# Row-wise infinity norm: the last 16 results of each partition leave in one store at the end, in place of an early store and a last one

## Chip, cores, metric

One NeuronCore of a Trainium2 chip. The metric is the device time of one execution in microseconds (us); lower is better. Before the change it was 628.59 us (median of 3 runs, 628.57 to 628.78).

## The reference

```python
x: float32 [8192, 8192]
return np.linalg.norm(x, ord=np.inf, axis=1)      # the largest |x| of each row
```

So 268.44 MB are read, 32 KB are written, and every element is looked at once.

## The kernel before

Each of the 128 partitions owns 64 rows. The first 48 of them ("bulk") come in 24 loads of two rows per partition; VectorE reduces each load to two numbers. The last 16 ("tail") come in loads of shrinking size, so that little is left to do when the last bytes arrive. All loads are issued by SP (the SyncE engine); ACT is ScalarE. A transfer reports its end by raising a semaphore, which engines wait for; "landing" below is the moment at which that semaphore is complete.

```python
TAIL = [[2944, 13440], [4096, 12288], [11520, 4864], ...,          # cut
        [2432, 2176, 1920, 1664, 1536, 1280, 1152, 1024, 1152, 1024, 1024]]
...
r_bulk = outp.tile([P, A, G * B], F32)
r_tail = outp.tile([P, n_tail], F32)           # n_tail = 16
r_fin = outp.tile([P, 1], F32)
part = outp.tile([P, n_tail - 1, k_max], F32)
nc.vector.memset(part[:], 0.0)
def absmax(o, i):
    nc.vector.reduce_max(out=o, in_=i, axis=X, apply_absolute_value=True)
...
nc.scalar.dma_start(out=out_b, in_=r_bulk[:])      # bulk results
for i, loads in enumerate(TAIL):
    t = sbuf.tile([P, W + PAD], F32, tag="t")
    ...
    for j, w in enumerate(loads):
        nc.sync.dma_start(out=t[:, at : at + w], in_=x_t[i][:, at : at + w])
        ...
            if r < n_tail - 1:
                absmax(part[:, r, k : k + 1], t[:, lo : lo + n])
                if r == n_tail - 2 and k == count[r] - 1:
                    absmax(r_tail[:, : n_tail - 1], part[:])
                    nc.scalar.dma_start(out=out_t[:, : n_tail - 1],
                                        in_=r_tail[:, : n_tail - 1])
            elif k < n_last - 1:
                absmax(t[:, W + k : W + k + 1], t[:, lo : lo + n])
            else:
                absmax(r_fin[:], t[:, lo : W + n_last - 1])
nc.sync.dma_start(out=out_t[:, n_tail - 1 :], in_=r_fin[:])
```

15 of a partition's tail results are combined and stored while the last row still arrives (128 runs of 60 bytes, on ACT's queue); the 16th is stored alone at the end (128 runs of 4 bytes, on SP's queue).

Of the kernel before, what the change touches and what calls it, by code (L numbers as in the profile page):

```python
# [1 line left out]
logging.getLogger("concourse").setLevel(logging.ERROR)  # L3

# [1 line left out]

# [4 lines left out]

F32 = mybir.dt.float32
X = mybir.AxisListType.X



TAIL = [
    [2944, 13440],
    [4096, 12288],
    [11520, 4864],  # L20
    [7680, 8704],
    [6528, 3328, 6528],
    [4864, 4096, 3328, 4096],
    [3968, 3584, 3328, 2944, 2560],
    [2432, 2176, 1920, 1664, 1536, 1280, 1152, 1024, 1152, 1024, 1024],
]


def segments(loads, cols):

    out, at = [], 0
    for i, w in enumerate(loads):
        end = at + w
        while at < end:
            r = at // cols
            to = min(end, (r + 1) * cols)
            out.append((i, r, at - r * cols, to - at))
            at = to
    return out


def start_first_load_early(nc):


    sp = mybir.EngineType.SP
    first, *rest = nc.main_func.blocks
    for block in rest:
        insts = block.instructions
        for i, ins in enumerate(insts):
            if ins.engine == sp and type(ins).__name__ == "InstDMACopy":  # L50
                assert not ins.sync_info.on_wait
                moved = insts[i]
                block.instructions = insts[:i] + insts[i + 1 :]
                head = first.instructions
                at = next(k for k, h in enumerate(head) if h.engine == sp)
                first.instructions = head[:at] + [moved] + head[at:]
                return


@with_exitstack  # L60
def kernel(
    ctx: ExitStack,
    tc: tile.TileContext,
    x: bass.AP,
    out: bass.AP,
    G: int = 4,
    B: int = 2,
    BUFS: int = 3,
    PAD: int = 16,
):  # L70
    nc = tc.nc
    P = nc.NUM_PARTITIONS
    rows, cols = x.shape
    W = B * cols


    n_tail = B * len(TAIL)
    n_bulk_rows = rows // P - n_tail
    assert n_bulk_rows % (G * B) == 0
    A = n_bulk_rows // (G * B)  # L80
    split = n_bulk_rows * P
    x_b = x[:split].rearrange("(a p n b) c -> a n p (b c)", p=P, a=A, n=G, b=B)
    out_b = out[:split].rearrange("(a p n b) -> p a (n b)", p=P, a=A, n=G, b=B)
    x_t = x[split:].rearrange("(p t b) c -> t p (b c)", p=P, b=B)
    out_t = out[split:].rearrange("(p t) -> p t", p=P)

    sbuf = ctx.enter_context(tc.tile_pool(name="sbuf", bufs=BUFS))
    outp = ctx.enter_context(tc.tile_pool(name="outp", bufs=1))

    segs = [segments(loads, cols) for loads in TAIL]  # L90
    count = {}
    for i, s in enumerate(segs):
        for _, r, _, _ in s:
            count[i * B + r] = count.get(i * B + r, 0) + 1
    n_last = count[n_tail - 1]
    k_max = max(count[r] for r in range(n_tail - 1))
    assert n_last - 1 <= PAD

    r_bulk = outp.tile([P, A, G * B], F32)
    r_tail = outp.tile([P, n_tail], F32)  # L100
    r_fin = outp.tile([P, 1], F32)
    part = outp.tile([P, n_tail - 1, k_max], F32)
    nc.vector.memset(part[:], 0.0)  # L103

    def absmax(o, i):
        nc.vector.reduce_max(out=o, in_=i, axis=X, apply_absolute_value=True)  # L106

    for a in range(A):
        for n in range(G):
            t = sbuf.tile([P, W + PAD], F32, tag="t")  # L110
            nc.sync.dma_start(out=t[:, :W], in_=x_b[a, n])
            absmax(
                r_bulk[:, a, n * B : (n + 1) * B],
                t[:, :W].rearrange("p (b c) -> p b c", b=B),
            )
    nc.scalar.dma_start(out=out_b, in_=r_bulk[:])

    seen = {}
    for i, loads in enumerate(TAIL):
        t = sbuf.tile([P, W + PAD], F32, tag="t")  # L120
        todo = segs[i]
        at = 0
        for j, w in enumerate(loads):
            nc.sync.dma_start(out=t[:, at : at + w], in_=x_t[i][:, at : at + w])  # L124
            at += w
            for _, b, c, n in [s for s in todo if s[0] == j]:
                r = i * B + b
                k = seen.get(r, 0)
                seen[r] = k + 1
                lo = b * cols + c  # L130
                if r < n_tail - 1:
                    absmax(part[:, r, k : k + 1], t[:, lo : lo + n])
                    if r == n_tail - 2 and k == count[r] - 1:

                        absmax(r_tail[:, : n_tail - 1], part[:])
                        nc.scalar.dma_start(
                            out=out_t[:, : n_tail - 1], in_=r_tail[:, : n_tail - 1]
                        )
                elif k < n_last - 1:
                    absmax(t[:, W + k : W + k + 1], t[:, lo : lo + n])  # L140
                else:

                    absmax(r_fin[:], t[:, lo : W + n_last - 1])
    nc.sync.dma_start(out=out_t[:, n_tail - 1 :], in_=r_fin[:])
    nc.at_finalize(start_first_load_early)


# [1 line left out]
_INS = ['x']  # L149
_OUTS = [((8192,), 'float32')]  # L150


# [23 lines left out]
```

## Time and profile before

| before | |
|---|---|
| time | 628.59 us |
| profiled span | 627.3 us |
| bytes over the span | 428 GB/s, DMA nine tenths busy or more in 39 of 40 slices |
| VectorE (DVE) busy | 88% |
| end of VectorE's last reduction | 625.02 us |
| from there to the end of the span | 2.29 us |

Lines of the page's first parts (others left out): busy time by engine, then forty slices of the span with the busy tenths of each engine and of the DMA.

```profile
span 627.3 us, 201 instructions
DVE 553.0 (88%) x64; POOL 0.2 (0%) x4
DVE  0688998888988889888898888998889999999998
DMA  9999999999999999999999999999999999999997
DMA packets 8994, 268.49 MB, mean 428 GB/s; under 512 B 1952, under 2 KB 1952, under 8 KB 3104
```

The DMA is full to the last slice, and VectorE is nearly full in the last quarter. How full, the windows show: start and end of a stretch, its length, DVE's busy time, then POOL, clock, DMA share and GB/s.

```profile
560.00:597.30 37.30, 37.10 (x11) 0.00 (x0) 1.00 1.00 426
597.30:615.70 18.40, 18.37 (x8) 0.00 (x0) 1.00 1.00 422
615.70:625.03 9.33, 9.26 (x8) 0.00 (x0) 1.00 0.74 300
625.03:627.30 2.27, 0.00 (x0) 0.00 (x0) 1.00 0.03 0
```

VectorE idles 0.1 us in the last 28 us of its work. The instructions of the end in order of time (start, duration, engine, line, operation, out<-in):

```profile
611.69 2.30 SPq L124 DMA_DIRECT2D t<-in_x_dram  x2
615.73 0.22 DVE L106 TENSOR_REDUCE r_tail<-part 128x15 f32<-128x60 f32 x1
615.86 7.90 DVE L106 TENSOR_REDUCE t<-t 128x1 f32<-128x1536 f32 x6
615.97 0.35 ACTq L136 DMA_DIRECT2D out_dram<-r_tail  x1
623.80 1.23 DVE L106 TENSOR_REDUCE r_fin<-t 128x1 f32<-128x1030 f32 x1
625.05 0.35 SPq L144 DMA_DIRECT2D out_dram<-r_fin  x1
```

The issues of stores, with KB and us from issue to landing:

```profile
out_dram<-r_bulk ACTq DMA_DIRECT2D x1, 24.0 KB, 60.1
out_dram<-r_tail ACTq DMA_DIRECT2D x1, 7.5 KB, 5.3
out_dram<-r_fin SPq DMA_DIRECT2D x1, 0.5 KB, 1.4
```

The early store (r_tail) overlaps VectorE's work and the loads. The last one (r_fin) begins when VectorE is done, and nothing overlaps it.

### The profile page before, as it was taken

To read this page: it belongs to the slowest core of one execution; us is meant where nothing else is said; L and a number is where in the kernel's file an instruction comes from. 1 tells how busy PE (TensorE), PEld (TensorE's weight loads), DVE (VectorE), ACT (ScalarE), POOL (GpSimd) and SP (SyncE) were. 2 spreads that over 40 slices of the span, in tenths; PEclk is the share of its full clock that TensorE was granted. 3 is DMA by queue.
4 is the path that set the end of the run, shared out by engine and by line. 5 is a ranking of instruction groups with operands and counts; after the bars stand their busy time and mean duration, and the time that the engine had idled before them with its cause. 6 is when DMAs were issued, how large, how long until landed. Compare 5 with 4: busy or idle time off the path is not lost.

```text
span 627.3 us, 201 instructions
## 1 busy us (share of the span) xinstructions
DVE 553.0 (88%) x64; POOL 0.2 (0%) x4
## 2 busy tenths in 40 slices
DVE  0688998888988889888898888998889999999998
POOL 0000000000000000000000000000000000000000
DMA  9999999999999999999999999999999999999997
GB/s 401 468 401 468 401 468 401 464 405 455 414 451 418 451 418 401 468 401 468 401 468 401 468 401 468 401 468 401 468 418 406 460 430 410 436 422 430 428 423 287
DMA packets 8994, 268.49 MB, mean 428 GB/s; under 512 B 1952, under 2 KB 1952, under 8 KB 3104
## 3 DMA queue, kind: packets, MB, share of 16 engines
q1 hardware_dynamic: 8064, 268.44, 99.3%
q10 hardware_dynamic: 928, 0.03, 0.1%
q14 instruction: 2, 0.02, 0.0%
HBM read 268.44 MB, written 0.03 MB: 428 GB/s over the span
## 4 chain that ended last, share of the span: by engine, by line
DMA 67%; DVE 28%; another core or an unknown queue 4%; SPq 0%; issue 0%
DMA t<-in_x_dram 67%; DVE r_bulk L106 22%; DVE part L106 5%; DVE t L106 1%; DVE r_fin L106 0%; SPq L124 0%; DVE r_tail L106 0%
## 5 line engine op out<-in xcount | busy, mean ns | idle before, releaser
L106 DVE TENSOR_REDUCE r_bulk<-t 128x2 f32<-128x16384 f32 x24 | 413.3, 17220 | 70.1 <-DMA t<-in_x_dram 70.1
L106 DVE TENSOR_REDUCE part<-t 128x1 f32<-128x8192 f32 (+18 forms) x31 | 130.5, 4273 | 0.9 <-DMA t<-in_x_dram 0.6
L106 DVE TENSOR_REDUCE t<-t 128x1 f32<-128x1152 f32 (+3 forms) x6 | 7.9, 1387 | 0.0
L106 DVE TENSOR_REDUCE r_fin<-t 128x1 f32<-128x1030 f32 x1 | 1.2, 1226 | 0.0
L103 DVE MEMSET part<- 128x60 f32 x1 | 0.1, 108 | 0.9 <-PEq L160 0.9
L106 DVE TENSOR_REDUCE r_tail<-part 128x15 f32<-128x60 f32 x1 | 0.2, 216 | 0.0
L160 POOL MEMSET const-bfloat16-1.0<- 128x1 bf16 x1 | 0.1, 103 | 0.0
L160 POOL MEMSET const-uint8-127<- 128x1 uint8 x1 | 0.1, 103 | 0.0
L160 POOL MEMSET const-float32-1.0<- 128x1 f32 x1 | 0.1, 100 | 0.0
L160 POOL MEMSET const-float32-0.0<- 128x1 f32 x1 | 0.1, 99 | 0.2 <-issue 0.2
## 6 DMA issues: line engine op xcount, KB each, us to landing
t<-in_x_dram SPq DMA_DIRECT2D x1, 6720.0 KB, 40.4
t<-in_x_dram SPq DMA_DIRECT2D x2, 3264.0 KB, 26.4
t<-in_x_dram SPq DMA_DIRECT2D x3, 2048.0 KB, 29.0
t<-in_x_dram SPq DMA_DIRECT2D x1, 6144.0 KB, 40.6
t<-in_x_dram SPq DMA_DIRECT2D x1, 5760.0 KB, 35.3
t<-in_x_dram SPq DMA_DIRECT2D x3, 1664.0 KB, 32.5
t<-in_x_dram SPq DMA_DIRECT2D x2, 2432.0 KB, 32.6
t<-in_x_dram SPq DMA_DIRECT2D x1, 4352.0 KB, 42.8
```

The costliest lines, as they stand in the source:

```text
L103: nc.vector.memset(part[:], 0.0)
L106: nc.vector.reduce_max(out=o, in_=i, axis=X, apply_absolute_value=True)
L160: nc = _bacc.Bacc("TRN2", target_bir_lowering=False, num_devices=1)
```

## The change

The intent: one store where there were two, in whole 64-byte runs, and no store among the last loads.

```diff
-    r_fin = outp.tile([P, 1], F32)
 ...
                         absmax(r_tail[:, : n_tail - 1], part[:])
-                        nc.scalar.dma_start(
-                            out=out_t[:, : n_tail - 1], in_=r_tail[:, : n_tail - 1]
-                        )
 ...
-                    absmax(r_fin[:], t[:, lo : W + n_last - 1])
-    nc.sync.dma_start(out=out_t[:, n_tail - 1 :], in_=r_fin[:])
+                    absmax(r_tail[:, n_tail - 1 :], t[:, lo : W + n_last - 1])
+    nc.sync.dma_start(out=out_t, in_=r_tail[:])
```

## The prediction

> **What bounds the kernel.** It streams 268.44 MB through 16 DMA engines: the page's slices show DMA at nine tenths or more in all but the last, 428 GB/s over the 627.3 us span. VectorE is 88% busy. In the bulk it waits about 2.1 us for each load (70.1 us in all, groups of instructions). From 519.67 us that turns: its tail reductions run nearly back to back (windows: 37.10 of 37.30 us from 560.0, 18.37 of 18.40 from 597.3, 9.26 of 9.33 from 615.7). So the end is VectorE's chain, then one store: the chain of waits ends with the 1.23 us reduction into r_fin at 623.80; the store issues at 625.05 (DMA issues: 1.4 us to landing; in the trace its first packet moves 0.85 us after the issue starts and its semaphore is complete at 626.30); then 1.0 us of closing semaphores and drains.
>
> **What the change does.**
> - Removed: the early store of 15 results (ACT's queue, 128 runs of 60 bytes, issued at 615.97, landed 5.3 us later, among the loads). No VectorE instruction waits for it. Its packets took 11 ns each, some 0.09 us on each of 16 DMA engines (estimate, 8 x 11 ns). The last load could land about 0.1 us earlier. It landed at 623.60, while VectorE was busy with the reduction before until 623.76: worth 0.
> - Moved: those 60 bytes into the last store. Same issuing engine, same 128 runs, 64 bytes each in place of 4. A 4-byte packet took 7 to 9 ns, a 60-byte one 11 ns; with 8 in series on each engine the store grows by an estimated 0.02 to 0.03 us, all on the critical path.
> - Unchanged: every reduction, also the 0.22 us one of the partial results, and the closing sequence. The last reduction writes column 15 of r_tail in place of r_fin: same shape, 1.23 us.
> - Side effect: completion semaphores are used in rotation (eight in the trace), so without the early store the last loads should each wait for a load one earlier, and issue up to 2 us sooner. The load queue is never empty there (410 to 422 GB/s from 616 to 622 us, windows): nothing gained.
>
> The Trainium skill ("DMA: Bandwidth & Descriptors", "Anatomy of one DMA") puts a small DMA's cost mostly in a fixed part, about 2 us, dominated by the write receipt. The trace agrees that it is fixed, at 1.24 us from issue to semaphore for 512 bytes, though most of that lies ahead of the first packet. The page's specifications say that transfers below 512 B are read-modify-written; 4, 60 and 64 bytes all are, so I expect little from longer runs: any gain must come out of the 0.2 us between last packet and semaphore.
>
> **Prediction.** +0.03 us for bytes, at most -0.05 us for whole pieces, 0 for the removed store. Time 628.6 us, 8 in 10 between 628.0 and 629.2. Chances: faster by over 2% 0.5%, within 2% 99%, slower by over 2% 0.5%.
>
> **What would show it.** Right: the last reduction ends within 0.2 us of 625.03; the last store takes 1.3 to 1.5 us to landing; packets under 512 B fall by 144 (128 data, 16 for the semaphore). Wrong: a last store of over 1.6 us, or VectorE finishing earlier (it did wait for disturbed loads).
>
> **What would make it wrong.** A load that lands later because issues move, so that VectorE waits at the end (slack is only 0.16 us at the last load); a last store that waits for something besides the last reduction; run-to-run drift, which at 628.57 to 628.78 exceeds the effect.

## The result

| | before | after |
|---|---|---|
| median, us | 628.63 (6 runs, 628.43 to 629.10) | 628.60 (6 runs, 628.33 to 629.41) |
| profiled span, us | 627.3 | 626.8 |

The ratio is 1.0001, with a 95% interval of 0.9988 to 1.0014: the same. (A ratio here is the mean time of one kernel's runs over that of the other's of the same rounds, so it isn't quite the ratio of the medians quoted.) Later the changed kernel ran again for five rounds: 0.9996 (0.9983 to 1.0008). The four that ran once (e5, e8, e9, e10): only stretches within their traces are read.

The profile after, the same views:

```profile
span 626.8 us, 199 instructions
DVE 552.9 (88%) x64; POOL 0.2 (0%) x4
DVE  0588988889988889888898888998889999999998
DMA  9999999999999999999999999999999999999997
DMA packets 8850, 268.49 MB, mean 428 GB/s; under 512 B 1808, under 2 KB 1808, under 8 KB 2960
```

```profile
611.24 0.33 SPq L123 DMA_DIRECT2D t<-in_x_dram  x1
615.27 0.22 DVE L105 TENSOR_REDUCE r_tail<-part 128x15 f32<-128x60 f32 x1
615.41 7.91 DVE L105 TENSOR_REDUCE t<-t 128x1 f32<-128x1536 f32 x6
623.35 1.23 DVE L105 TENSOR_REDUCE r_tail<-t 128x1 f32<-128x1030 f32 x1
624.60 0.35 SPq L140 DMA_DIRECT2D out_dram<-r_tail  x1
```

```profile
out_dram<-r_tail SPq DMA_DIRECT2D x1, 8.0 KB, 1.4
```

VectorE is as full in the stretch before the last row as it was before the change, and the only wait for a tail load that the view lists is the same early one of 0.6 us (total us, times, longest):

```profile
597.30:615.70 18.40, 18.37 (x10) 0.00 (x0) 1.00 1.01 423
DVE part L105 <- DMA t<-in_x_dram: 0.6, 1, 0.6
```

Small packets fell by 144 (1952 to 1808), as they should: 128 of data and 16 for a semaphore. The last store takes 1.4 us, with sixteen times the bytes. The profiled span is 0.51 us shorter, but that is not the change's doing: the first tail reduction starts 0.27 us sooner (484.02 against 484.29 us), more than 100 us ahead of the first instruction that differs; another 0.18 us arises in VectorE's short waits for loads between there and the last reduction, and is scatter: from the first tail reduction to the end of the last took 140.74 us before and 140.56 after, but 140.45 in a later run with the early store (e1_both) and 140.70 in one without it (e6_bulk_late). Only 0.06 us lies behind the last reduction (2.23 us to the end of the span in place of 2.29). What those 0.06 us are is a question that the prediction had not foreseen.

### The profile page after: what moved, and what is told of

Read it like the earlier page. It is cut to its first block, busy times and chain, and to the rows that moved or that the text cites. A ratio compares the mean times of both kernels' runs of the same rounds, so it can differ in the third digit from the quotient of the medians.

```text
span 626.8 us, 199 instructions
## 1 busy us (share of the span) xinstructions
DVE 552.9 (88%) x64; POOL 0.2 (0%) x4
## 2 busy tenths in 40 slices
DMA packets 8850, 268.49 MB, mean 428 GB/s; under 512 B 1808, under 2 KB 1808, under 8 KB 2960
## 4 chain that ended last, share of the span: by engine, by line
DMA 67%; DVE 28%; another core or an unknown queue 4%; SPq 0%; issue 0%
DMA t<-in_x_dram 67%; DVE r_bulk L105 22%; DVE part L105 5%; DVE t L105 1%; DVE r_tail L105 0%; SPq L123 0%
```

## The experiments

Twelve kernels ran. Exact intervals below are differences of the trace's records; "behind the last reduction" is from the end of VectorE's last reduction to the end of the span.

**The theory.** VectorE's chain sets when the last store starts; the early store only delays loads, within VectorE's slack at the last load; the last store has a fixed cost, and its bytes weigh 0.02 us. **Rivals**: (1) two effects cancel, a gain from dropping the early store and a cost of the wider last one; (2) whole 64-byte runs land faster than 4-byte ones; (3) stores among the loads are free whatever their size.

### One half of the change at a time

The control, the changed kernel itself (e0_after):

> Control: the changed kernel again, in the rounds of the next three. Both theories: 628.6 us, within 0.15% of the kernel before. In its trace the last store takes 1.4 us to landing.

Measured: 628.56 us against 628.71 us of before on that chip, ratio 0.9996.

Both stores, with the last one wide (e1_both), against the changed kernel:

```diff
+                        nc.scalar.dma_start(
+                            out=out_t[:, : n_tail - 1], in_=r_tail[:, : n_tail - 1]
+                        )
```

> The early store of 15 results is kept, and the last store carries all 16 (64-byte runs). Theory (both halves are worth about nothing): within 0.15% of before; from the end of the last reduction to the end of the span 2.25 to 2.35 us, as in before (2.28) and after (2.24). Rival 1 (two effects cancel: the wider last store costs what the dropped early store gains): slower than before, with the span's end over 0.2 us later after the last reduction. Rival 2 (whole 64-byte pieces land faster than 4-byte ones): last store under 1.2 us to landing in place of 1.4.

Measured: 628.62 us, ratio 0.9998 (0.9985 to 1.0010).

Only the early store dropped (e2_no_early), against the kernel before; its output is wrong:

```diff
-                        nc.scalar.dma_start(
-                            out=out_t[:, : n_tail - 1], in_=r_tail[:, : n_tail - 1]
-                        )
```

> The early store is dropped and the last stays at 4-byte runs, so 15 of the 16 tail rows are never written: wrong on purpose. Theory: within 0.15% of before; the last load lands 0.2 to 0.3 us before VectorE is done with the reduction ahead of the last (0.17 in before), and VectorE does not use it. Rival 1: faster by what the early store cost, with VectorE's last reduction ending over 0.2 us sooner after the combining reduction's start (9.31 us in before).

Measured: 628.62 us, ratio 0.9998 (0.9984 to 1.0012). The four kernels side by side, from the traces:

| | early store | last store, bytes a run | last load lands ahead of VectorE by | issue to last semaphore step | behind the last reduction |
|---|---|---|---|---|---|
| before | yes | 4 | 0.17 us | 1.41 us | 2.29 us |
| e1_both | yes | 64 | 0.16 us | 1.41 us | 2.30 us |
| e2_no_early | no | 4 | 0.26 us | 1.42 us | 2.23 us |
| after | no | 64 | 0.24 us | 1.41 us | 2.23 us |

This settles most of it. Each effect goes with one half of the change and does not depend on the other, so nothing cancels (rival 1 falls). The width of the last store makes no difference that can be seen (rival 2 falls for 128 runs). Dropping the early store brings the last load about 0.08 to 0.09 us forward, which is the 0.09 us that the prediction estimated from 8 packets of 11 ns, and VectorE, still at the reduction before, does not use it. (The last load is also issued 2 us sooner without the early store, and these runs do not part the two. But it lies in the queue for 9.9 us before and 11.8 us after, from issue to landing, with the DMA full, so the earlier issue can hardly be what brought it forward.) And the 0.06 us behind the last reduction go with the early store, not with the width.

### Ten times the dose of the early store

```diff
+                        nc.scalar.dma_start(      # scr: a scratch tensor in HBM; t_prev: the tile before
+                            out=scr.rearrange("p (r k) -> p r k", k=512)[:, :4, :256],
+                            in_=t_prev[:, :2048].rearrange("p (r k) -> p r k", k=512)[:, :, :256],
+                        )
```

> The kernel before with a second early store on ACT's queue, of 512 KB (128 partitions x 4 runs of 1 KB) into a scratch tensor: the early store's suspected cost, transport on the 16 engines, at some ten times the dose. Theory (a store among the loads delays the last load by its transport time, and costs what exceeds VectorE's slack of 0.17 us): 32 runs of about 40 ns on each engine, the last load 0.8 to 1.3 us later, VectorE idle 0.6 to 1.1 us in the tail, 629.3 to 629.7 us. Rival 3 (a store among the loads is off the critical path whatever its size): 628.6 us and no idle time of VectorE in the tail.

Measured: 629.92 us against 628.71, ratio 1.0018 (1.0006 to 1.0031). The schedule issued the store at 588.5 us, earlier than intended, since its source was ready. VectorE's waits of this run, and those of before:

```profile
DVE part L106 <- DMA t<-in_x_dram: 1.7, 5, 0.6
```

```profile
DVE part L106 <- DMA t<-in_x_dram: 0.6, 1, 0.6
```

(total us, times, longest.) VectorE waits 1.1 us more for loads, in four pieces between 597 and 608 us (0.43, 0.20, 0.21 and 0.22 us). So a store among the loads is not free, and rival 3 falls. An estimate of its transport is 1.23 us (0.52 MB at the 425 GB/s of that stretch), and nearly all of it reached VectorE: at 597 us VectorE had no backlog to hide it.

The store had a second effect, though. SP's next load shared its semaphore, and SP waited 13.6 us for it, from 593.2 us on, before issuing any more loads. That could have starved the DMA, but did not: in those 13.6 us the DMA share was 1.02 at 424 GB/s (1.01 and 425 before). So the delay is put down to transport. The measured time is 0.2 us over the expected range; the store was placed where there is no slack at all, and 0.1 us of it is behind the last reduction (2.39 us), for which see the section after next. The 60-byte store was harmless by its size and place, not by its kind.

### How far the last reduction is from its load

The combining reduction (0.22 us) is left out, so 15 tail rows leave as zeros, wrong (e7_no_combine):

```diff
+    nc.vector.memset(r_tail[:], 0.0)
 ...
-                        absmax(r_tail[:, : n_tail - 1], part[:])
+                        pass
```

> The changed kernel without the combining reduction of 0.22 us, so that 15 tail rows leave as zeros: wrong on purpose. Theory (the tail is VectorE's chain, with the last load only 0.17 to 0.24 us ahead of it): the last reduction ends 0.15 to 0.22 us sooner after the start of the first reduction of the last row, measured from the landing of the last load it starts 0.0 to 0.1 us after it; 628.4 us, not clear of noise in the times. Rival 6 (the tail waits for loads): no reduction ends sooner.

Measured: 628.39 us, ratio 0.9993 (0.9978 to 1.0008), not clear of noise. The trace:

```profile
615.26 5.53 DVE L106 TENSOR_REDUCE t<-t 128x1 f32<-128x1536 f32 x4
621.26 2.48 DVE L106 TENSOR_REDUCE t<-t 128x1 f32<-128x1152 f32 x2 [0.47 <-DMA t<-in_x_dram]
623.77 1.23 DVE L106 TENSOR_REDUCE r_tail<-t 128x1 f32<-128x1030 f32 x1
```

VectorE now runs into a load that isn't there yet and waits 0.47 us. Its last reduction starts 0.10 us after the last load's landing, as expected, and ends 1.33 us after it, in place of 1.50 us in the changed kernel: 0.17 us, not 0.22. The other measure, from the first reduction of the last row, is 0.57 us longer and was badly chosen: in this run that reduction itself started early and the wait came behind it. So rival 6 is half right: loads and VectorE end within about 0.2 us of each other. In the last row, taking 0.22 us of work from VectorE alone gained 0.17 us, and taking the early store's 0.09 us from the loads alone (e2_no_early) gained nothing.

### What the 0.06 us are

The closing sequence on SP waits for the loads' and stores' semaphores, eight in rotation, in fixed pairs, one instruction each. SP's closing waits in the trace of before and of after (start in us, duration in ns, the two semaphores):

```
before                        after
625.451   28  104, 103        625.003   28  104, 103
625.520   28  105, 102        625.072   28  105, 102
625.587  898  106, 101        625.139   28  106, 101
626.522   28  107, 100        625.203  837  107, 100
```

In the changed kernel the last store has semaphore 100, in the last pair; before, the early store had taken a place in the rotation, the last store got 101, and after its landing one more wait had to be gone through. (In the run with two early stores it had 102, two waits before the end, and 2.39 us; 0.03 us of these are the store itself, which took 1.44 us.) If that is all, the 0.06 us have nothing to do with the stores. Two runs turn it round, each by changing the number of loads:

```diff
 e9_one_load_more, against the changed kernel:
-    [11520, 4864],
+    [5760, 5760, 4864],
 e10_one_load_less, against the kernel before:
-    [2944, 13440],
+    [16384],
```

> The changed kernel with one tail load cut in two, so that the last store's semaphore is the one the kernel before used for it (the second of the rotation). The question: why do the runs without an early store end 2.23 us after the last reduction and those with it 2.29 us. Theory (the closing waits go through the semaphores in fixed pairs, and the early store only moved the last store's semaphore out of the last pair, so that one more wait of 0.06 us follows its landing): 2.29 us, without any early store. Rival (the early store itself lengthens the end): 2.23 us.

> The kernel before, early store and 4-byte last store included, with its first two tail loads joined, so that the last store's semaphore is in the last pair of the closing waits. Theory: 2.23 us from the end of the last reduction to the end of the span, in place of 2.29. Rival: 2.29.

Measured: 2.29 us without an early store (semaphore 101), and 2.23 us with it (semaphore 100). The rotation decides, and the rival falls. All 14 traces agree: from the completion of the last semaphore to the end of the span it is 0.79 us where that semaphore is 100, 0.85 to 0.86 us where it is 101, and 0.92 to 0.93 us where it is 102. (One time each, 628.62 and 629.16 us; not compared, as the loads differ.)

### What runs and bytes cost in a last store

Sixteen times the runs (e3_short_runs): the results lie 8 bytes apart on chip, so each leaves on its own.

```diff
-    r_tail = outp.tile([P, n_tail], F32)
+    r_tail = outp.tile([P, n_tail, 2], F32)
 ...
-    nc.sync.dma_start(out=out_t, in_=r_tail[:])
+    nc.sync.dma_start(out=out_t, in_=r_tail[:, :, 0])
```

> The changed kernel with the results spaced 8 bytes apart on chip, so that the last store leaves in 2048 runs of 4 bytes in place of 128 of 64: 128 on each engine in place of 8. Theory (a run costs 7 to 11 ns on its engine, in series, on top of a fixed cost of 1.2 us): the last store takes 2.1 to 2.6 us to landing in place of 1.4, and the kernel is 0.8 to 1.3 us slower (629.4 to 629.9). Rival 4 (bytes or the fixed cost decide, not runs): 1.4 us and 628.6 us.

Measured: 642.71 us against 628.99, ratio 1.0219 (1.0204 to 1.0235). The added 13.7 us are more than ten times the 0.8 to 1.3 us expected; rival 4, which expected no cost at all, falls too. Who waited, and where:

```profile
out_dram<-r_tail SPq DMA_DIRECT2D x1, 8.0 KB, 15.7
SPq L167 <- DMA out_dram<-r_tail: 14.8, 1, 14.8
```

The packets were through 2.6 us after the issue, as the theory wanted; but the semaphore was complete only at 15.7 us. So something follows the packets that no packet record shows. Two series of stores, one after another and meant for an otherwise idle DMA, measured it, each in one run. The first (e5_ladder) varies the length of 128 runs:

```diff
     nc.sync.dma_start(out=out_t, in_=r_tail[:])
+    scr = nc.dram_tensor("scr", (128, 16384), F32, kind="Internal").ap()
+    for n in (1, 15, 16, 64, 128, 256, 1024, 4096):
+        nc.sync.dma_start(out=scr[:, :n], in_=t[:, :n])
```

> The changed kernel, then eight stores into a scratch tensor, one after another on an otherwise idle DMA, of 4, 60, 64, 256, 512, 1024, 4096 and 16384 bytes in each of 128 runs. Theory: 4, 60, 64 and 256 bytes land within 0.1 us of each other, at about 1.25 us from issue to semaphore; a step, if there is one, only by transport (512 KB: 1.2 us more). Rival 2 (pieces that must be read, modified and written are slow): 4 and 60 bytes land over 0.15 us later than 64 bytes, or everything under 512 bytes later than 512.

Measured, from issue to the last step of the semaphore: 60 bytes 1.40 us, 64 bytes 1.45 (beside the kernel's own store), 256 bytes 1.47, 512 bytes 1.52, 1024 bytes 1.65, 4096 bytes 2.56, 16384 bytes 6.21. The schedule issued the first two ahead of the kernel's own store: the 60-byte one at 623.8 us, just behind the landing of the last load, and the 4-byte one at 613.7 us among the loads, where it took 10.1 us, so that it says nothing for an idle DMA. In this series the runs lie 64 KB apart in HBM (the off-chip memory). Among the other lengths there is no step at 512 bytes, only transport. (The theory had 1.25 us for the level: see "A misreading" below.)

The second (e8_shapes; r_w holds the 16 results and zeros) brings the 4-byte store behind the last load and varies the number and the neighbourhood of runs; all stores wait for the last reduction:

```diff
+    for o, i in (
+        (flat(16), r_w[:, :16]),               # 128 x 64 B, beside the kernel's own store
+        (flat(16)[:, :1], r_w[:, 15:16]),      # 128 x 4 B
+        (flat(16)[:, :15], r_w[:, 1:16]),      # 128 x 60 B
+        (flat(16), r_w[:, :16]),               # 128 x 64 B
+        (step(16, 1)[:, :, 0], src[:, :, 0]),  # 2048 x 4 B, 4 B apart in HBM
+        (step(16, 2)[:, :, 0], src[:, :, 0]),  #             8 B
+        (step(16, 16)[:, :, 0], src[:, :, 0]), #            64 B
+        (step(16, 128)[:, :, 0], src[:, :, 0]),#           512 B
+        (step(16, 16), src[:, :, :16]),        # 2048 x 64 B, side by side
+        (step(6, 8), src[:, :6, :8]),          # 768 x 32 B, side by side
+    ):
+        nc.sync.dma_start(out=o, in_=i)
```

> The changed kernel, then ten stores of results one after another into a scratch tensor on an otherwise idle DMA: 128 runs of 64 (a first one, beside the kernel's own last store), 4, 60 and 64 bytes at a step of 64; 2048 runs of 4 bytes at steps of 4 (as in the run with short runs), 8, 64 and 512 bytes; 2048 runs of 64 bytes side by side; 768 runs of 32 bytes side by side. Theory A (neighbouring pieces of one 64-byte line are written one after the other, each waiting for the one before): 2048 x 4 bytes at step 4 takes 13 to 16 us, at step 8 about half or more of that, at steps of 64 and 512 about 2.5 us. Theory B (a short write costs about 0.1 us on its engine wherever it goes): 13 to 16 us at all four steps, and the 128 runs of 4 or 60 bytes, 8 on each engine, cost up to 0.8 us more than those of 64. Either way 128 runs of 4, 60 and 64 bytes within 0.1 us of each other at about 1.25 us speak for the prediction's sum; 2048 runs of 64 bytes near 2.5 us.

| store, runs x bytes | step in HBM | last packet ends after | semaphore complete after | rest |
|---|---|---|---|---|
| 128 x 4 | 64 B | 1.01 us | 1.45 us | 0.4 us |
| 128 x 60 | 64 B | 1.03 us | 1.70 us | 0.7 us |
| 128 x 64 | 64 B | 1.03 us | 1.42 us | 0.4 us |
| 2048 x 4 | 4 B | 2.54 us | 13.76 us | 11.2 us |
| 2048 x 4 | 8 B | 2.46 us | 9.46 us | 7.0 us |
| 2048 x 4 | 64 B | 2.46 us | 5.37 us | 2.9 us |
| 2048 x 4 | 512 B | 2.46 us | 4.13 us | 1.7 us |
| 2048 x 64 | 64 B | 2.48 us | 3.16 us | 0.7 us |
| 768 x 32 | 32 B | 1.70 us | 2.21 us | 0.5 us |

Three of these as the profile's list of DMA issues has them (KB, us to landing), in stretches around the 4-byte stores at steps of 4 and 512 bytes and around the 64-byte runs:

```profile
scr<-r_w SPq DMA_DIRECT2D x1, 8.0 KB, 13.8
scr<-r_w SPq DMA_DIRECT2D x1, 8.0 KB, 4.1
scr<-r_w SPq DMA_DIRECT2D x1, 128.0 KB, 3.2
```

Up to the last packet only the number of runs counts: 128 on each engine take 1.3 us from first packet to last, about 10 ns each, whether they carry 4 or 64 bytes. What follows depends on where short pieces go: 11.2 us for neighbours, 2.9 us at a step of 64 bytes, 1.7 us at 512. Theory A had the trend and the first two sizes, but not the last two (it put steps of 64 and 512 at 2.5 us in all); theory B, one cost wherever they go, falls. Why short pieces cost more when they share their surroundings isn't shown by any record. For 128 runs, 4 and 64 bytes are 0.02 us apart. The 60-byte store is 0.3 us late here, against the expectation of 0.1 us at most, and was not in the first series (1.40 us, but with its runs 64 KB apart in place of 64 bytes); its cause stays open.

### The same change carried further

If one late store costs nothing, could the bulk results leave at the end as well? They would spare a store whose semaphore SP is seen waiting for, 25 us long (before):

```profile
SPq L124 <- DMA out_dram<-r_bulk: 25.1, 1, 25.1
```

First try (e6_bulk_late), the bulk store's line moved behind the last one:

```diff
-    nc.scalar.dma_start(out=out_b, in_=r_bulk[:])
 ...
     nc.sync.dma_start(out=out_t, in_=r_tail[:])
+    nc.scalar.dma_start(out=out_b, in_=r_bulk[:])
```

> The change carried further: the 48 bulk results of a partition also leave at the very end (768 runs of 32 bytes, on ACT's queue beside the last store on SP's). Theory: 48 more runs on each engine at about 10 ns add some 0.4 to 0.6 us behind the last reduction; the 25 us for which SP waited on the early bulk store go, but the DMA was full in them (433 GB/s), so they give nothing back: 629.0 to 629.3 us. Rival 5 (that wait held the loads up): faster than 628 us.

Measured: 628.91 us, ratio 0.9997 (0.9980 to 1.0014). It tested nothing: the store only waits for the bulk results, ACT has nothing else to do, and the schedule left it at 484.5 us, with the same semaphore and the same wait. Second try (e11_bulk_last), where a one-element operation ties the bulk results to the last reduction:

```diff
-    nc.scalar.dma_start(out=out_b, in_=r_bulk[:])
 ...
+    nc.vector.scalar_tensor_tensor(
+        out=r_bulk[:, 0, 0:1], in0=r_tail[:, n_tail - 1 :], scalar=0.0,
+        in1=r_bulk[:, 0, 0:1], op0=mybir.AluOpType.mult, op1=mybir.AluOpType.add,
+    )
     nc.sync.dma_start(out=out_t, in_=r_tail[:])
+    nc.scalar.dma_start(out=out_b, in_=r_bulk[:])
```

> The run with the late bulk store built again so that it really leaves last: a one-element VectorE operation behind the last reduction writes back one bulk result (times zero plus itself), and the bulk store of 768 runs of 32 bytes waits for it. Theory: the small operation 0.1 to 0.2 us, then the store about 2.2 us to landing (its time in the run of store shapes) in place of 1.4, so 0.8 to 1.2 us more behind the last reduction (3.0 to 3.4 us to the end of the span in place of 2.23); in front nothing comes back from the 25 us for which SP waited on the early bulk store, but for a store's transport of 0.4 us off the loads: 629.0 to 629.8 us. Rival 5 (that wait held the loads up): faster than 628 us.

```profile
624.70 0.35 SPq L143 DMA_DIRECT2D out_dram<-r_tail  x1
624.71 0.16 DVE L139 SCALAR_TENSOR_TENSOR r_bulk<-r_tail,r_bulk 128x1 f32<-128x1 f32 x1
624.90 0.42 ACTq L144 DMA_DIRECT2D out_dram<-r_bulk  x1
```

Measured: 629.25 us against 628.68, ratio 1.0009 (0.9996 to 1.0023), and 3.02 us behind the last reduction in place of 2.23. The store took 2.0 us (768 x 32 bytes: 2.2 us in the series). The 0.8 us are paid at the end, as reckoned. The 25 us wait is gone and brought nothing visible: from the first tail reduction to the end of the last it is 140.49 us here, 140.56 after, 140.74 before and 140.45 in the run with both stores, which is scatter. So rival 5 falls as well. No experiment points to a version that beats both kernels by anything the times could show.

## Why the prediction was right

- **The sum.** Predicted 628.6 us, measured 628.60 us; nothing gained, nothing lost. That holds at the level of single steps, too: each half of the change alone leaves the time where it was.
- **"Worth 0" for the dropped early store.** Shown. It does bring the last load forward, by 0.08 to 0.09 us (predicted about 0.1), and VectorE is busy at that moment.
- **"+0.02 to 0.03 us" for the bytes.** Not seen. The packets of the last store span 0.207 us in place of 0.199, and the semaphore comes at 1.413 us in place of 1.411. But with 4 bytes e2_no_early has 0.203 and 1.416 us, so not even the sign can be read.
- **"At most -0.05 us for whole pieces".** Nothing of it is seen: at 128 runs, 4 and 64 bytes land alike.
- **The side effect.** The last load is issued 4.04 us ahead of the combining reduction in place of 2.07, the predicted 2 us sooner, and it gained nothing. But the rotation of semaphores had a second consequence that the prediction missed: the last store's place among the closing waits, worth 0.06 us, which is more than either term that it did reckon.
- **A sign that failed.** The prediction wanted the last reduction to end within 0.2 us of 625.03 us, and named an earlier end as a sign that it was wrong. It ended at 624.58 us. The sign was badly chosen, for the point scatters by more than that: it lies at 624.43 us in the control (e0_after) and at 625.08 us in e6_bulk_late, which ran on the same schedule. The other two signs held (1.4 us to landing, 144 packets fewer).
- **A misreading.** The prediction took the first step of the last store's semaphore (1.24 us after the issue, at 626.30 us) for its completion. The semaphore goes up in 16 steps and is complete 1.41 us after the issue, at 626.46 us. So what follows the last packet is 0.37 us, not 0.2, and the closing sequence 0.85 us, not 1.0 (0.79 after the change, by the rotation). The sum did not suffer, since the prediction took both parts as unchanged.
- **The Trainium skill's fixed cost** ("DMA: Bandwidth & Descriptors", "Anatomy of one DMA", about 2 us, mostly the write receipt): its table is for DMAs issued through GpSimd, which the prediction left out; here, from SP, it is 1.41 us, of which 0.84 lie ahead of the first packet and 0.37 behind the last. What follows the last packet, where the receipt would be looked for, is thus the smaller part for 128 small runs; for 2048 neighbouring runs of 4 bytes it is 11.2 of 13.8 us. No record shows the receipt itself. The page's specifications say that transfers below 512 bytes are read-modify-written; no run shows whether these stores were, and for 128 runs no step in time was seen at 512 bytes (1.47 us at 256 bytes, 1.52 at 512).

## What to carry to other kernels

In this kernel a last store of a few bytes per partition costs its fixed 1.4 us, and one run of 64 bytes per partition costs no more than one of 4; so the number of stores and their width are worth changing only if a run's count or the critical path changes with them. Before taking a small store out from among the loads, look at what waits for the load behind it: here 0.09 us of transport fell into 0.25 us of slack and left 0.17 us, while ten times the dose, in a place without slack, was paid nearly in full. And do not let results leave as single 4-byte pieces side by side: 2048 of them cost 14 us here.

## What the Trainium skill lacked or had wrong

- "DMA: Bandwidth & Descriptors", "Rules for kernel authors", says that a non-contiguous last dimension lowers to one descriptor per element and to rearrange; it gives no cost for what follows the last packet of such a store. Here 2048 pieces of 4 bytes took 13.8 us side by side, 5.4 us at a step of 64 bytes, 4.1 us at 512, and 2048 runs of 64 bytes 3.2 us; the packets had ended after 2.5 us in all of them.
- The same page, "Specifications", names 512 bytes as the bound below which transfers are read-modify-written. With 128 runs, 256, 512 and 1024 bytes landed at 1.47, 1.52 and 1.65 us (one run, pieces 64 KB apart): no step in time there, and the page does not say how large one should be.
- The same page, "Anatomy of one DMA", has this breakdown of the fixed cost for DMAs issued by GpSimd only (about 2.0 us). From SP, a store of 512 bytes in 128 runs took 1.41 us from issue to the last step of the semaphore.
- No page that was read says that the place of the last transfer in the rotation of semaphores sets how many closing waits follow its landing: 2.23, 2.29 and 2.39 us behind the last reduction, with zero, one and two waits to go (0.79, 0.85 and 0.92 us from the last semaphore's completion).
